# Queries' sums of squares by products with a column of ones, and an earlier load of the scan's levels, in a hybrid delta/SGU/Fourier step

## The chip, the cores and the metric

One Trainium2 chip, one core used. The metric is the device time of one execution in microseconds (us), the median of several runs.

## The reference

One layer of a flow-matching backbone on 2048 sample tokens and 128 prompt tokens, D_MODEL 1024. One input projection feeds three mixers of width 512: a gated delta rule (A, 4 heads of 128), a spatial gating unit (B) and a Fourier mix (C). Each is gated, projected, weighted by a sigmoid merge gate, summed and projected out. What the change touches is branch A:

```python
def l2norm(x):
    return x * lax.rsqrt(jnp.sum(x * x, axis=-1, keepdims=True) + EPS)
...
q = l2norm(q.reshape(B, T, H_A, DK)) * (DK ** -0.5)
k = l2norm(k.reshape(B, T, H_A, DK))
...
m = eye + bc[..., :, None] * jnp.einsum('bnhik,bnhjk->bnhij', kc, kc) * dec_strict
sol = lax.linalg.triangular_solve(m, rhs, left_side=True, lower=True, unit_diagonal=True)
def step(s, inp):
    u = u0_ - jnp.einsum('bhck,bhkv->bhcv', w_, s)
    o = jnp.einsum('bhck,bhkv->bhcv', qg_, s) + jnp.einsum('bhij,bhjv->bhiv', qk_, u)
    s = gl_[..., None, None] * s + jnp.einsum('bhck,bhcv->bhkv', kd_, u)
...
pb = jnp.einsum('btnw,nwd->btnd', br, w_branch)
merged = jnp.einsum('btnd,btnd->btd', gt, pb)
```

## The kernel before, in words

TensorE runs one long stream of matrix products: the input projection by column blocks, then the merges n = 1, 2, 0 of the three branches, then the output projection. Nearly all products are float16, each float32 operand split into a high and a low part and three products taken (`mm3`). Their instructions all stand on line 250.

Branch A is woven into that stream. `Pace` gives it a step whenever enough of the main stream has been issued. It works in chunks of 128 tokens, 17 in all, in 5 groups (the prompt's chunk, then four of four chunks):

- `prep` (lines 1007 to 1094, 437 to about 800 us in the profile) takes a chunk's q, k and v, which lie with the head's 128 channels on the partitions. It turns k, v and q by transposes on TensorE (line 1016; 4 of each, one for a head), sums squares over the channels on ScalarE (line 1022), takes the inverse root on GpSimd (line 1024), scales k into `tok`, turns `tok` back (line 1049), and makes the Gram matrices in float16.
- `base_inverse` (line 1101 on) inverts the 32 x 32 diagonal blocks of a group's triangular systems in 31 rounds between VectorE (line 1114, tile XB) and GpSimd (line 1115, tile E), then stores the result (`ei`).
- `scan` runs both directions over the chunks, 34 steps. For each chunk `level` builds the full inverse R from the 32-blocks: it loads `ei` into the tile ES and the Gram matrix into N and sn (lines 1171 to 1177, DMAs on SyncE's queue), and then multiplies in four steps: ES with N, ES with Q, T with sn, R with Q. ES, N and Q exist once and are shared by all levels. A step of the scan has its own products: S with the turned k (sk), v with R, u with k (kn), and those of the output (`attend`). Generators `lev` (the level of the next chunk), `nlev` (the one after) and `att` are advanced by `next` at fixed places of a step.

At the same time `gate_unit` finishes a block of branch B or C: a product on GpSimd (line 1465, tile st), a square on ScalarE (line 1466) and a store from GpSimd's queue (line 1467, br). Weights are converted ahead (lines 315, 327, 328: squares and both halves). In a merge, `branch_block` loads the branch's rows (tile st, three buffers) and converts them into `big` (lines 1691 and 1692).

The order of instructions on each engine is not that of the code: a scheduler with a model of the engines sorts them, so an edit at one place moves rows at others behind it. Names in rows read out<-moving, stationary for a product; a number behind a name is that of a buffer.

Of the kernel before, what the change touches and what calls it, by code (L numbers as in the profile page):

```python
# [14 lines left out]
AF = mybir.ActivationFunctionType  # L15
ALU = mybir.AluOpType
# [4 lines left out]
P = 128  # L21
# [6 lines left out]
H = 4  # L28
WB = 512
EPS = 1e-6  # L30
# [164 lines left out]
def hybrid_flow_kernel(ctx: ExitStack, tc: tile.TileContext, x_prompt, x_sample, state_delta, c, c_ctx, w_ada,  # L195
# [4 lines left out]
    G, V, A, PE = [_InTurn(tc, e_) for e_ in (nc.gpsimd, nc.vector, nc.scalar, nc.tensor)]  # L200
# [9 lines left out]
    def sb(pl, shape, tag, dt=F32, bufs=None):  # L210
        kw = {} if bufs is None else {"bufs": bufs}
        return pl.tile(list(shape), dt, tag=tag, name=nm(tag), **kw)
# [6 lines left out]
    ps_d = [pool(ctx, f"ps_d{i}", 1, space=PSUM) for i in range(3)]  # L219
# [4 lines left out]
    def bank(pl, shape, tag="b"):  # L224
        if pl is ps_d:
            rot[0] += 1
            pl = ps_d[rot[0] % 3]
        return pl.tile(list(shape), F32, tag=tag, name=nm(tag))
# [9 lines left out]
    ident, ones = K["ident"], K["ones"]  # L238
# [10 lines left out]
    def mm(out, l, r, start=True, stop=True, reopened=False):  # L249
        newest[0] = PE.matmul(out, l, r, start=start, stop=stop, skip_group_check=reopened)  # L250
# [453 lines left out]
    for ti, (t0, tn) in enumerate(TBS):  # L704
        g = 0 if t0 < NS else 1
# [13 lines left out]
        for k in range(KT):  # L719
            x, hi, _ = part_of(k)  # L720
# [91 lines left out]
    dq = pool(dl, "dqa", 1, side="right")  # L812
# [172 lines left out]
    def rows(part, t):  # L985
        x = sb(d2, [P, H, P], "kq" if part else "qr", bufs=3 if part else 2)
        SY.dma_start(x, qkvD[part * 4:part * 4 + 4, :, chunk_off(t):chunk_off(t) + P].rearrange("h p t -> p h t"))
        return x
# [18 lines left out]
    def prep(g, ci, t, nxt, held):  # L1007

        tok = sb(dq, [P, 2, WB], "tok")
        ss = sb(dq, [P, 2, H], "ss2", bufs=2)  # L1010
        cur = dict(held)

        def turned(part):
            ps = bank(ps_d, [P, WB])
            for h in range(H):
                PE.transpose(ps[:, hs(h)], cur[part][:, h, :], ident)
            return ps

        def norm(ps, i):
            sq = sb(dq, [P, WB], "sq")  # L1020
            for h in range(H):
                A.activation(sq[:, hs(h)], ps[:, hs(h)], AF.Square, accum_out=ss[:, i, h:h + 1])
            V.tensor_scalar(ss[:, i, :], ss[:, i, :], EPS, None, ALU.add)
            G.tensor_tensor(ss[:, i, :], ss[:, i, :], mhalf.to_broadcast([P, H]), ALU.pow)  # L1024

        def more(key, make):
            if nxt is not None:
                held[key] = make()

        more(1, lambda: rows(1, nxt))  # L1030
        ps = turned(1)
        norm(ps, 1)
        V.tensor_tensor(h3(tok[:, 0, :]), h3(ps), bc(ss[:, 1, :], P), ALU.mult)
        yield 1
        more(0, lambda: rows(0, nxt))
        A.activation(tok[:, 1, :], turned(2), AF.Copy, scale=us)
        norm(turned(0), 0)
        G.tensor_scalar(rq[:, t, :], ss[:, 0, :], P ** -0.5, None, ALU.mult)
        Q16 = sb(d2, [P, 2, WB], "q16", F16)
        qr = cur[0].rearrange("p h x -> p (h x)")  # L1040
        made = A.activation(Q16[:, 0, :], qr, AF.Copy, scale=qs)
        V.scalar_tensor_tensor(Q16[:, 1, :], qr, qs, Q16[:, 0, :], ALU.mult, ALU.subtract)
        late([(qTD[t], Q16)], made)
        yield 1
        G.dma_start(kvD[t], tok)
        T = sb(d2, [P, 2, WB], "T", F16)
        ps = bank(ps_d, [P, WB])
        for h in range(H):
            PE.transpose(ps[:, hs(h)], tok[:, 0, hs(h)], ident)
        made = A.activation(T[:, 0, :], ps, AF.Copy, scale=FS)  # L1050
        V.scalar_tensor_tensor(T[:, 1, :], ps, FS, T[:, 0, :], ALU.mult, ALU.subtract)
        more(2, lambda: rows(2, nxt))
        late([(kTD[t], T)], made)
        yield 1
        dc = cur["dc"]
        ps = bank(ps_d, [P, WB])
        pair = lambda t_, h: (t_[:, 0, hs(h)], t_[:, 1, hs(h)])
        for h in range(H):
            mm3(ps[:, hs(h)], pair(T, h), pair(T, h))
        nd = sb(d2, [P, 2, H, 32], "nd", bufs=2)  # L1060
        for d in range(2):
            n_ = sb(d2, [P, WB], "n32", bufs=3)
            for h in range(H):
                V.scalar_tensor_tensor(n_[:, hs(h)], ps[:, hs(h)], beta[:, d, t, h:h + 1], dc[:, d, hs(h)], ALU.mult, ALU.mult)  # L1064
            for B in range(4):
                A.copy(nd[32 * B:32 * B + 32, d], h3(n_)[32 * B:32 * B + 32, :, 32 * B:32 * B + 32])  # L1066
            n16 = sb(d2, [P, 2, WB], "n16", F16, bufs=4)
            made = A.activation(n16[:, 0, :], n_, AF.Copy, scale=FS)
            V.scalar_tensor_tensor(n16[:, 1, :], n_, FS, n16[:, 0, :], ALU.mult, ALU.subtract)
            late([(nD[d][t], n16)], made)  # L1070
            yield 1
        more("dc", lambda: decay_rows(nxt))
        for d in range(2):
            G.dma_start(ndD[g][d, ci].rearrange("h p i -> p h i"), nd[:, d])
        ps = bank(ps_d, [P, WB])
        for h in range(H):
            mm3(ps[:, hs(h)], pair(T, h), pair(Q16, h))
        for d in range(2):
            q_ = sb(d2, [P, WB], "n32", bufs=3)
            V.tensor_mul(q_, ps, dc[:, d, :])  # L1080
            p16 = sb(d2, [P, 2, WB], "n16", F16, bufs=4)
            made = A.activation(p16[:, 0, :], q_, AF.Copy, scale=1.0 / FS)
            V.scalar_tensor_tensor(p16[:, 1, :], q_, 1.0 / FS, p16[:, 0, :], ALU.mult, ALU.subtract)  # L1083
            late([(qkD[d][t], p16)], made)
            yield 1
# [171 lines left out]
    def scan():  # L1257
# [31 lines left out]
        for i_, (d, s_, t) in enumerate(order):  # L1289
# [18 lines left out]
            yield 1  # L1308
            next(att, None)
            yield 1  # L1310
            next(nlev, None)
            yield 1
            next(lev, None)
            yield 1
            next(att, None)
            yield 1
# [11 lines left out]
            split(u, v_)  # L1328
            yield 1
            next(nlev, None)  # L1330
            yield 1
            next(att, None)
            yield 1
# [18 lines left out]
                split(S216, S2, 1.0 / FS)  # L1352
            yield 1
            next(nlev, None)
            lev, nlev = nlev, level(*order[i_ + 2][::2]) if i_ < 32 else iter(())
            loaded = step_loads(i_ + 1)
            R3 = next(nlev, None)
            yield 1
            yield 1
            for _ in att:  # L1360
# [322 lines left out]

    def branch_block(n, s, t0, tn):

        for g in range(4):
            st = sb(ep, [P, tn], "st", bufs=3)
            SY.dma_start(st, obD[n][g, :, t0:t0 + tn])
            yield
            with behind_gate():  # L1690
                A.activation(o16[:, 0, g, t0:t0 + tn], st, AF.Copy, scale=s)  # L1691
            V.scalar_tensor_tensor(o16[:, 1, g, t0:t0 + tn], st, s, o16[:, 0, g, t0:t0 + tn], ALU.mult, ALU.subtract)  # L1692
# [490 lines left out]
```

## Time and profile before

| | |
|---|---|
| time, median of 3 runs | 2151.89 us (2148.55 to 2152.83) |
| profiled execution | 2150.54 us |
| its span | 2148.7 us, mean granted TensorE clock 0.99 |
| TensorE busy | 2085.8 us (97%) |
| VectorE busy | 1328.0 us (62%) |
| ScalarE busy | 1062.1 us (49%) |
| GpSimd busy | 840.1 us (39%) |

TensorE (PE) is busy nearly all the time; what is not its work is its idle time of some 60 us and the stretches in which its clock is granted at half. PEld is the load of the stationary operand, which overlaps the products. A busy share is an average over the whole span, so stages are read apart, by windows.

### The profile page before, as it was taken

The page shows a single profiled execution, that of the slowest core. Times are in us where ns is not written, and L with a number is a line of the kernel's source. Part 1 is how long each engine was busy: PE and PEld are TensorE (multiplying, and loading weights), DVE is VectorE, ACT ScalarE, POOL GpSimd, SP SyncE. Part 2 cuts the span into 40 slices and gives each one's busy share as a digit, 9 for nine tenths or more (in the row PEclk, how much of TensorE's full clock was granted, in tenths as well). Part 3 has the DMA queues.
Part 4 walks back from the last instruction along what each step waited for, and adds up shares of the span by engine and source line. Part 5 has one row for each costly group of instructions (what it writes and reads, how often), then busy time and mean ns, then how long its engine had stood idle before and what let it go on. Part 6 is the DMA issues. An engine that isn't in the chain of part 4 may idle for free.

```text
span 2148.7 us, 42636 instructions
## 1 busy us (share of the span) xinstructions
PE 2085.8 (97%) x16133; PEld 1198.8 (56%) x16133; DVE 1328.0 (62%) x2945; ACT 1062.1 (49%) x2457; POOL 840.1 (39%) x1089
## 2 busy tenths in 40 slices
PE   8999999999999999999899999999999999999997
PEld 4454444455555677787555655555655444444443
DVE  6656854388777786466655555766665564666245
ACT  5554744465656664455544445655554353443112
POOL 0321342225565555542322233255443234343464
PEclk9999999999999999999999999999999999999999
DMA  9525722177877743444655556866664645456852
GB/s 353 220 77 186 270 102 102 68 222 232 260 227 245 222 142 95 118 139 136 203 183 170 161 167 187 252 214 210 211 204 131 210 165 176 167 196 237 339 220 88
DMA packets 222909, 403.24 MB, mean 188 GB/s; under 512 B 39720, under 2 KB 109632, under 8 KB 219888
## 3 DMA queue, kind: packets, MB, share of 16 engines
q1 hardware_dynamic: 167664, 290.84, 42.3%
q0 software_dynamic: 15216, 65.89, 8.1%
q10 hardware_dynamic: 39824, 43.79, 6.0%
q8 instruction: 127, 2.08, 0.4%
q14 instruction: 78, 0.64, 0.1%
HBM read 258.19 MB, written 142.24 MB: 186 GB/s over the span
## 4 chain that ended last, share of the span: by engine, by line
PE 50%; DVE 8%; DMA 7%; POOL 3%; ACT 3%; issue 3%; SPq 0%; ACTq 0%; DVEq 0%; POOLq 0%
PE b L250 50%; DMA st<-br 2%; DMA pa<-pa 1%; DMA ES<-ei 1%; POOL E L1115 1%; DVE XB L1114 1%; DVE big L1692 1%; ACT nd L1066 1%; POOL ss L1024 1%; POOL st L1465 0%; ACT big L1691 0%; DVE n L1083 0%; DMA wst<-in_w_blk_dram 0%; DVE sg L476 0%; DVE n L1064 0%
## 5 line engine op out<-in xcount | busy, mean ns | idle before, releaser
L250 PE MATMUL b<-xh,whi 128*128 128x512 f16 (+1 forms) x1920 | 650.4, 348 | 2.9 <-DVE sg L1455 1.8
L250 PE MATMUL b<-xl,whi 128*128 128x512 f16 (+1 forms) x1920 | 650.6, 347 | 0.0
L250 PE MATMUL b<-xh,wlo 128*128 128x512 f16 (+1 forms) x1920 | 649.4, 347 | 0.0
L250 PEld LDWEIGHTS <-whi 128*128 128x128 f16 x3856 | 351.7, 98 | 322.6 <-issue 7.5
L250 PEld LDWEIGHTS <-wlo 128*128 128x128 f16 x1928 | 188.7, 98 | 176.7 <-issue 2.2
L250 PE MATMUL b<-big,bhi 128*128 128x512 f16 (+1 forms) x960 | 251.1, 347 | 1.7 <-ACT big L1691 1.1
L250 PE MATMUL b<-big,blo 128*128 128x512 f16 (+1 forms) x480 | 163.0, 347 | 0.0
L1735 POOL TENSOR_TENSOR mrow<-mrow,sg 128x512 f32<-128x512 f32 (+1 forms) x80 | 93.4, 1169 | 146.2 <-DVE sg L1734 115.4
L953 POOL TENSOR_TENSOR cy<-cy,raw 128x545 f32<-128x545 f32 (+1 forms) x48 | 64.4, 1368 | 183.6 <-ACT raw L952 183.6
L250 PEld LDWEIGHTS <-xh 128*128 128x128 f16 x1496 | 117.0, 98 | 28.8 <-issue 1.4
L250 PEld LDWEIGHTS <-bhi 128*128 128x128 f16 x960 | 86.7, 98 | 76.6 <-issue 2.6
L1115 POOL TENSOR_TENSOR E<-E,XB 128x31 f32<-128x31 f32 (+15 forms) x155 | 94.0, 607 | 84.6 <-DVE XB L1114 67.8
L250 PEld LDWEIGHTS <-xl 128*128 128x128 f16 x1068 | 98.1, 98 | 44.9 <-DMA tw<-tw 1.4
L1725 ACT ACTIVATE sg<-b,winv 128x512 f32<-128x512 f32 (+1 forms) x120 | 74.0, 616 | 94.0 <-PE b L250 93.4
L1188 POOL COPY T<-ES 32x256 f16<-32x256 f16 x68 | 32.1, 473 | 174.5 <-DMA ES<-ei 159.1
L250 PE MATMUL b<-whi,xh 128*128 128x128 f16 x544 | 92.7, 219 | 0.0
L250 PE MATMUL b<-whi,xl 128*128 128x128 f16 x544 | 92.7, 219 | 0.0
L250 PE MATMUL b<-wlo,xh 128*128 128x128 f16 x544 | 92.7, 219 | 0.0
L328 DVE SCALAR_TENSOR_TENSOR wlo<-wst,wsc,whi 128x1024 f16<-128x1024 f32 x52 | 69.9, 1346 | 31.4 <-ACT whi L327 31.1
L1295 POOL TENSOR_TENSOR skn<-skn,ed 128x512 f32<-128x512 f32 x34 | 37.2, 1095 | 122.5 <-DMA skn<-kv 122.5
L315 ACT ACTIVATE wlo<-wst 128x1024 f16<-128x1024 f32 x52 | 54.9, 1056 | 58.2 <-DMA wst<-in_w_blk_dram 54.8
L1114 DVE TENSOR_TENSOR XB<-XB,E 128x31 f32<-128x31 f32 (+15 forms) x155 | 55.3, 357 | 41.7 <-POOL E L1115 41.1
(532 smaller groups left out, 4314.8 us busy)
## 6 DMA issues: line engine op xcount, KB each, us to landing
wst<-in_w_blk_dram SPq DMA_DIRECT2D x58, 512.0 KB, 4.7
pa<-pa POOLq DMA_DIRECT2D x16, 896.0 KB, 4.4
qkv<-cy POOLq DMA_DIRECT2D x12, 1089.0 KB, 5.3
st<-br SPq DMA_DIRECT2D x48, 256.0 KB, 2.9
mrow<-mrg SPq DMA_DIRECT2D x16, 576.0 KB, 4.2
pa<-pa SPq DMA_DIRECT2D x5, 1792.0 KB, 11.9
dc<-dec SPq DMA_DIRECT2D x17, 512.0 KB, 4.7
kq<-qkv SPq DMA_DIRECT2D x34, 256.0 KB, 5.3
```

Of the source, the lines that this page charges most:

```text
L250: newest[0] = PE.matmul(out, l, r, start=start, stop=stop, skip_group_check=reopened)
L315: w.squared = A.activation(w.lo, st, AF.Square, accum_out=ss)
L328: w.low = V.scalar_tensor_tensor(w.lo, st, s, w.hi, ALU.mult, ALU.subtract)
L953: G.tensor_tensor(y[:, c0:c1], y[:, c0:c1], raw[:, 1 + c0:1 + c1], ALU.mult)
L1024: G.tensor_tensor(ss[:, i, :], ss[:, i, :], mhalf.to_broadcast([P, H]), ALU.pow)
L1066: A.copy(nd[32 * B:32 * B + 32, d], h3(n_)[32 * B:32 * B + 32, :, 32 * B:32 * B + 32])
L1114: V.tensor_tensor(t3, X3[:, 0:k, k:k + 1].to_broadcast([P, k, n_]), E3[:, k:k + 1, k:32].to_broadcast([P, k, n_]), ALU.mult)
L1115: G.tensor_tensor(E3[:, 0:k, k:32], E3[:, 0:k, k:32], t3, ALU.subtract)
L1188: G.tensor_copy(T16[rows(a0, b), :, :, b], ES[0:32, :, 2 * a0 + b, :, wT])
L1295: G.tensor_tensor(h3(kn_), h3(kn_), bc(ed[:, d, t, :], P), ALU.mult)
L1725: gated_[0] = A.activation(sg, ps, AF.Sigmoid, scale=gw.inv)
L1735: G.tensor_tensor(mr, mr, sg, ALU.add)
```

## The change: what it does

Three edits.

1. In `prep`, q is no longer turned. ScalarE squares the 512 columns of q as loaded, in one instruction, into `q2`. TensorE then multiplies each head's squares (as the stationary operand, float32) by one column of ones, which sums over the channels, into a PSUM tile of 128 x 4. VectorE reads the sums there. The squares of k are dumped into the still unused half of `tok` instead of a tile of their own.
2. In the scan's step, `next(lev)` comes ahead of `next(nlev)` at one place, and the level two chunks ahead is set up (its loads are issued) behind the split of u instead of at the step's end.
3. In `branch_block`, three rows are loaded at once, and the fourth after the first conversion.

```diff
         def norm(ps, i):
-            sq = sb(dq, [P, WB], "sq")
             for h in range(H):
-                A.activation(sq[:, hs(h)], ps[:, hs(h)], AF.Square, accum_out=ss[:, i, h:h + 1])
-            V.tensor_scalar(ss[:, i, :], ss[:, i, :], EPS, None, ALU.add)
+                A.activation(tok[:, 1, hs(h)], ps[:, hs(h)], AF.Square, accum_out=ss[:, i, h:h + 1])
+            inverse_root(ss[:, i, :], i)
+
+        def inverse_root(sums, i):
+            V.tensor_scalar(ss[:, i, :], sums, EPS, None, ALU.add)
             G.tensor_tensor(ss[:, i, :], ss[:, i, :], mhalf.to_broadcast([P, H]), ALU.pow)
...
+        qr = cur[0].rearrange("p h x -> p (h x)")
+        q2 = sb(dq, [P, WB], "sq")
+        A.activation(q2, qr, AF.Square)
         ps = turned(1)
         norm(ps, 1)
...
-        norm(turned(0), 0)
+        ps = bank(ps_d, [P, H])
+        for h in range(H):
+            mm(ps[:, h:h + 1], q2[:, hs(h)], ones[:, 0:1])
+        inverse_root(ps, 0)
...
+            next(lev, None)
+            yield 1
             next(nlev, None)
-            yield 1
-            next(lev, None)
...
             next(nlev, None)
+            later = level(*order[i_ + 2][::2]) if i_ < 32 else iter(())
+            R3 = next(later, None)
...
-            lev, nlev = nlev, level(*order[i_ + 2][::2]) if i_ < 32 else iter(())
+            lev, nlev = nlev, later
             loaded = step_loads(i_ + 1)
-            R3 = next(nlev, None)
...
-        for g in range(4):
+        def loaded(g):
             st = sb(ep, [P, tn], "st", bufs=3)
             SY.dma_start(st, obD[n][g, :, t0:t0 + tn])
-            yield
+            return st
+
+        sts = [loaded(g) for g in range(3)]
+        yield
+        for g in range(4):
+            if g == 1:
+                sts.append(loaded(3))
+            st = sts[g]
```

The scheduler moves rows elsewhere too. Three places matter below. In the steady scan the engines' rows stay nearly as they were, two groups of products changing places; the loads of ES stay where they were on SyncE's queue, since they wait for the products that read ES.

First, GpSimd's queue at the end of the last inverse before the scan (E are the rounds of the inverse, st and br the product and store of a branch block). Before:

```order
L1115 TENSOR_TENSOR E_9690<-E_9690,XB_9689 128x4x28
L1465 TENSOR_TENSOR st_10527<-sg_10172,yT_9570 128x512
L1465 TENSOR_TENSOR st_10531<-sg_10231,yT_9570 128x512
L1465 TENSOR_TENSOR st_10535<-sg_10329,yT_9570 128x512
L1115 TENSOR_TENSOR E_9690<-E_9690,XB_9689 128x3x29
L1467 DMA br_3917<-st_10527 128x512
L1467 DMA br_3917<-st_10531 128x512
L1467 DMA br_3917<-st_10535 128x512
L1115 TENSOR_TENSOR E_9690<-E_9690,XB_9689 128x2x30
L1465 TENSOR_TENSOR st_10567<-sg_10564,yT_9570 128x512
L1465 TENSOR_TENSOR st_10599<-sg_10596,yT_9570 128x128
L1115 TENSOR_TENSOR E_9690<-E_9690,XB_9689 128x31
```

After:

```order
L1122 TENSOR_TENSOR E_9622<-E_9622,XB_9621 128x4x28
L1122 TENSOR_TENSOR E_9622<-E_9622,XB_9621 128x3x29
L1122 TENSOR_TENSOR E_9622<-E_9622,XB_9621 128x2x30
L1122 TENSOR_TENSOR E_9622<-E_9622,XB_9621 128x31
L1473 TENSOR_TENSOR st_10459<-sg_10104,yT_9502 128x512
L1473 TENSOR_TENSOR st_10463<-sg_10163,yT_9502 128x512
L1473 TENSOR_TENSOR st_10467<-sg_10261,yT_9502 128x512
L1475 DMA br_3917<-st_10459 128x512
L1475 DMA br_3917<-st_10463 128x512
L1475 DMA br_3917<-st_10467 128x512
L1144 MEMSET R_1255_10436 128x1024
```

The last rounds now run together, and the branch products and stores follow them. On TensorE, the first product of ES and N stands some 11 us of work earlier than before.

Second, TensorE's queue at the end of the first level's products of ES and Q. Before, the second level's product of ES and N is next:

```order
L250 MATMUL b_10903<-ES_10512,Q_1274_10508 128x64
L250 LDWEIGHTS Q_1274_10508
L250 MATMUL b_10903<-ES_10512,Q_1274_10508 128x64
L250 LDWEIGHTS N_1275_10510
L250 MATMUL b_11169<-ES_10512,N_1275_10510 128x32
```

After, other products follow, and the second level's product of ES and N comes 124 products later:

```order
L250 LDWEIGHTS Q_1257_10440
L250 MATMUL b_10835<-ES_10444,Q_1257_10440 128x64
L250 LDWEIGHTS xl_95
L250 MATMUL b_10933<-whi_9606,xl_95 128x128
L250 LDWEIGHTS xh_94
L250 MATMUL b_10933<-whi_9606,xh_94 128x128
```

So between the last reader of the first ES and the first reader of the second, TensorE now has other work: 56 products of 128 columns of the main stream, 16 of 512 columns, 24 of 128 and 3 of 256 of the Fourier mix, 12 each of T with sn and R with Q, and one of a single column.

Third, ScalarE's queue at the start of the first merge (S is the split of the scan's state, blo the square of a branch weight). Before:

```order
L327 ACTIVATE bhi_13438<-wst_11441,wsc_13445 128x512
L1297 CAST kn_1551_13567<-skn_13530 128x512
L315 ACTIVATE blo_13787,bsums_93<-wst_13634 128x512
L1231 ACTIVATE S_1544_13513<-S_11074 128x512
L1725 ACTIVATE sg_13557<-b_13489,winv_12257 128x512
```

After:

```order
L327 ACTIVATE bhi_13381<-wst_11373,wsc_13388 128x512
L1304 CAST kn_1534_13499<-skn_13473 128x512
L1238 ACTIVATE S_1528_13456<-S_11006 128x512
L315 ACTIVATE blo_13730,bsums_93<-wst_13566 128x512
L1740 ACTIVATE sg_13489<-b_13432,winv_12189 128x512
```

S has moved ahead of the square of the weight.

1 line of the change is left out of this document (removed).

## The prediction

> **What bounds the kernel now.** I read the page's first and fourth parts first, to see which engine sets the time.
>
> ```profile
> PE 2085.8 (97%) x16133; PEld 1198.8 (56%) x16133; DVE 1328.0 (62%) x2945; ACT 1062.1 (49%) x2457; POOL 840.1 (39%) x1089
> PE 50%; DVE 8%; DMA 7%; POOL 3%; ACT 3%; issue 3%; SPq 0%; ACTq 0%; DVEq 0%; POOLq 0%
> ```
>
> TensorE works 97% of the span. Only two things can move the end: the amount of work that TensorE gets, and its idle time. The windows view shows where that idle time lies, and at what granted clock (the columns are the window, its length, then busy us of PE, PEld, DVE, ACT and POOL, then PEclk, the DMA share and GB/s).
>
> ```profile
> 437.00:795.00 358.00, 353.56 (x2762) 216.85 (x2761) 285.03 (x702) 224.74 (x687) 192.30 (x278) 1.00 0.71 224
> 795.00:895.00 100.00, 96.12 (x1314) 80.19 (x1314) 62.44 (x148) 43.89 (x95) 54.59 (x88) 0.98 0.36 104
> 895.00:965.00 70.00, 61.39 (x784) 48.96 (x783) 40.76 (x100) 34.18 (x84) 34.95 (x57) 0.90 0.46 135
> 1015.00:1085.00 70.00, 62.15 (x523) 36.92 (x522) 47.47 (x118) 39.66 (x88) 20.98 (x32) 0.95 0.66 208
> 1085.00:1340.00 255.00, 255.00 (x2338) 152.61 (x2336) 141.94 (x384) 117.15 (x287) 72.44 (x110) 1.00 0.55 169
> 1340.00:1420.00 80.00, 72.59 (x634) 42.74 (x632) 55.71 (x138) 52.67 (x136) 33.95 (x42) 1.00 0.75 235
> ```
>
> The reader is to see four places. The preparation of the delta rule runs from 437 to 795 with 4.4 us of idle time in 358. The scan starts at about 895: 8.6 us idle in 70, at a mean clock of 0.90, so about 7 us more are lost. The first merge starts at about 1015: 7.9 us idle at 0.95, some 3.5 us more lost. From 1085 to 1340 the scan runs with no idle at all, and at the change from the first merge to the second (1340 to 1420) 7.4 us are idle again. The waits view names what ended some of it (total, times, longest, in us).
>
> ```profile
> PE b L250 <- DMA ES<-ei: 5.9, 2, 3.7
> PE b L250 <- ACT S L1231: 4.0, 3, 2.3
> PE b L1049 <- DVE tok L1033: 2.7, 3, 1.5
> PE b L250 <- DVE sg L1455: 1.8, 1, 1.8
> PE b L250 <- ACT big L1691: 1.1, 2, 0.7
> ```
>
> **Part 1: the sums of squares of the queries.** Before, each of the 17 chunks turns q by four transposes, and ScalarE squares the result in four pieces. After, ScalarE squares q once, unturned, and TensorE multiplies the four heads' squares, as stationary operands, by one column of ones. First ScalarE's side, from the groups of line 1022 and, for one 512-column square, of line 1466:
>
> ```profile
> L1022 ACT ACTIVATE sq<-b x136: 252/277/337, 440.2 to 793.9; 128x128 f32<-128x128 f32 x136
> L1022 ACT ACTIVATION_READ_ACCUMULATOR sq<-b x136: 188/211/272, 440.3 to 794.1; 128x1 f32 x136
> L1466 ACT ACTIVATE sg<-st x40: 292/630/686, 553.8 to 1037.4; 128x512 f32<-128x512 f32 x32, 128x128 f32<-128x128 f32 x8
> ```
>
> ScalarE loses 4 × (0.277 + 0.211) = 1.95 us a chunk and gains 0.63, so 17 × 1.32 = 22 us of its busy time go. It was busy for 225 of the 358 us, so this is taken from an engine with slack. I count it at nothing directly; its indirect use is below. TensorE's side is what counts, since TensorE has no slack there:
>
> ```profile
> L1016 PE MATMUL b<-cst,qr x68: 272/273/279, 440.4 to 792.0; 128*128 128x128 f32 x68
> L182 PE MATMUL b<-cst,rs x34: 272/275/377, 21.2 to 131.1; 128*128 128x128 f32 x34
> 609.84 1.04 PE L1016 MATMUL b<-cst,kq 128*128 128x128 f32 x8
> 610.71 0.60 PE L1016 MATMUL b<-cst,qr 128*128 128x128 f32 x4
> 611.15 0.38 PE L250 MATMUL b<-xh,whi 128*128 128x512 f16 x1
> 164.92 0.84 PE L250 MATMUL b<-tok,cst 128*128 128x68 f32 x6
> 165.60 0.38 PE L250 MATMUL b<-xl,whi 128*128 128x512 f16 x1
> ```
>
> A transpose is one record (68 for 17 chunks of 4). A true float32 product is two: the spread of the root (line 182, tile rs) is one product a chunk, and has 34 records for 17. The durations of 0.27 us overlap, so I take the distance from start to start. Twelve transposes take 611.15 − 609.84 = 1.31 us, 0.109 each, so q's four cost 0.44. Six records of the float32 products at 164.92 take 0.68 us, 0.113 each, most of them with only 68 moving columns. Fewer columns did not make them cheaper, which points at the load of the 128 stationary columns as the limit. Four new products are eight records: 8 × 0.113 = 0.90. The difference is 0.46 us a chunk, and 17 × 0.46 = **+7.8 us** of work on TensorE. The low bound is 0, if a one-column record takes half as long as a 68-column one; a high one is +10, if a chain of such small products also leaves gaps of 0.1 us.
>
> The Trainium skill, on the page "TensorE: Matmul & The Clock Gate", section "LDWEIGHTS (loading the stationary operand)", speaks against this edit in the same way: the load of a stationary operand takes its columns divided by 1.2 GHz whatever the other side is, so 0.107 us for 128; by it the term would be 17 × (0.85 − 0.44) = 7.1 us, an estimate. The trace's 0.109 and 0.113 agree with it, and no run here shows a one-column float32 product.
>
> What cover is there? In this stretch 4.4 us of idle time exist. The waits on tok (2.7 in all, some of it just past 795) and on sg (1.8) belong to it. The new products stand between the transposes of k, which tok comes from, and the transposes of tok, so they fill about half a microsecond of each such wait; ScalarE's shorter queue brings the sums for k earlier. I take −2 us for both (0 to −4), and −1 for the clock right behind, which dips to 0.98 after 795 (0 to −2).
>
> **Part 2: the scan's levels.** In the steady scan (1085 to 1340) TensorE is never idle, and the new order there swaps two neighbouring groups of about 2 us. I count nothing (within ±1). At the start of the scan it is different:
>
> ```profile
> 900.65 0.18 PE L250 MATMUL b<-ES,N 128*128 128x32 f16 x1 [0.55 <-POOL T L1188]
> 906.13 0.28 PE L250 MATMUL b<-ES,Q 128*128 128x64 f16 x4
> 910.07 0.47 PE L250 MATMUL b<-ES,N 128*128 128x32 f16 x8 [3.66 <-DMA ES<-ei]
> 916.31 0.39 PE L250 MATMUL b<-v,R 128*128 128x128 f16 x2 [1.32 <-ACT R L1203]
> 937.12 0.45 PE L250 MATMUL b<-ES,N 128*128 128x32 f16 x8 [2.20 <-DMA ES<-ei]
> 925.22 1.22 PE L250 MATMUL b<-cf,X 128*128 128x128 f16 x19
> 926.28 0.38 PE L250 MATMUL b<-xh,whi 128*128 128x512 f16 x1
> 926.50 0.38 PE L250 MATMUL b<-xl,whi 128*128 128x512 f16 x1
> ```
>
> ES is one buffer. Its second load can only start when the products of ES and Q at 906 have read the first, and before the next product stands right behind them: hence 3.66 us. In the new order some 9.7 us of other products stand between: 16 of 512 columns at 0.215 us (926.28 to 926.50), three of half that width, and 105 narrow ones at 0.056 (19 in the 1.06 us from 925.22). That covers the 3.66. The 1.32 at v,R goes too, since R,Q now stands further ahead, and of the 2.20 perhaps half. So 6 of the 8.6 us can go.
>
> Against it stands the first product of all. It now comes about 11 us of TensorE work earlier, and what it needs does not come as much earlier:
>
> ```profile
> 869.95 3.75 POOL L1465 TENSOR_TENSOR st<-sg,yT 128x512 f32<-128x512 f32 x3 [0.54 <-DVE yT L1641]
> 876.45 1.69 POOL L1465 TENSOR_TENSOR st<-sg,yT 128x512 f32<-128x512 f32 x2 [0.51 <-DMA br<-st]
> 878.10 0.25 POOL L1115 TENSOR_TENSOR E<-E,XB 128x31 f32<-128x31 f32 x1
> 888.80 0.95 POOL L1137 MEMSET R<- 128x1024 f16 x1 [9.39 <-DMA ei<-XB]
> 894.71 2.55 SPq L1171 DMA_DIRECT2D ES<-ei  x3
> 899.76 0.83 POOL L1188 COPY T<-ES 32x256 f16<-32x256 f16 x2 [3.17 <-DMA ES<-ei]
> ```
>
> The chain is: the rounds of E on GpSimd end at 878.4, the store of ei is awaited for 9.39 us, six clears follow, ES is asked for at 894.7 and is there at 899.8. In the new order the rounds of E come ahead of the branch products that held them for 3.75 us from 869.95 on and for 1.69 from 876.45 on, each with the DMA issues behind it. That brings the chain 5 to 7 us forward. So the first product, 11 us earlier by work, waits 0.55 + 11 − 6, about 5 us. Net idle time: 8.6 − 6 + 4.5, about 7. The clock may gain more, since one wait replaces four in 40 us; of the 7 us lost to it I let 4.5 go. Together I take **−6 us** (from −12, where the chain gains all that the product does, to +3, where it gains nothing).
>
> The Trainium skill has a rule on the same page, "TensorE: Matmul & The Clock Gate", section "Part 1: The HAM clock gate": TensorE falls to half clock after about 3.4 us of idleness, so one wait of 5 us would be followed by a slow stretch. The 3.66 us wait with its mean clock of 0.90 agrees. It is the weight behind the second rival.
>
> **At the start of the first merge** the order changes as a by-product. ScalarE's queue there:
>
> ```profile
> 1030.96 0.63 ACT L315 ACTIVATE blo<-wst 128x512 f16<-128x512 f32 x1 [3.03 <-DMA wst<-in_w_brb_dram]
> 1032.25 0.22 PE L250 MATMUL b<-S,sk 128*128 128x128 f16 x1 [2.27 <-ACT S L1231]
> ```
>
> The scan's state S stood behind a weight conversion that waited 3.03 us for its transfer. In the new order S comes ahead of it, and the 2.27 us go. The other waits in this stretch are of 0.1 to 1.5 us and will fall anew. I take −2.5 (from −6, where the clock's 3.5 us lost there go too, to +4).
>
> **Part 3: the branch tiles.** There were and are three buffers. The waits view of line 1691 shows what the conversions wait for:
>
> ```profile
>   DMA st<-br: 33.6, 26
> ```
>
> ScalarE waits 33.6 us, but TensorE waits for it only 1.1 us (above). A load can still start only when a buffer is free, and in the new order SP's rows for these loads are almost where they were. I take −0.3 (from −1.1 to +1). At the change between merges (1340 to 1420) the end of the scan is now interleaved with the conversions a little differently: 0, from −3 to +4.
>
> **The sum** is +7.8 − 2 − 1 − 6 − 2.5 − 0.3 = −4.0. The profiled execution took 2150.54 us, with 2148.7 of span, so it gives 2146.5. The median shown is 1.35 us above the profiled run; half of that added gives **2147 us**. That is 0.2% under the median, at the border of what a measurement of this kernel can tell from no change (0.2%, 4.3 us).
>
> **The rivals.** Forecast (chance 0.42): as above, its own range 2143 to 2151. About half of it is faster by over 0.2%, half within.
>
> Slower: the first product's wait (0.28). TensorE pays the full +7.8 at 437 to 795, and at the scan's start the first product's wait takes back what the others give: if the chain to ES comes forward by 2 us and not 6, this wait is 9.5 us, idle time becomes 8.6 − 6 + 9, about 11.6, and the clock's loss stays at 7. That is +3 there, −2 at the waits in preparation and the merge at 0: 2150.5 + 7.8 + 3 − 2, about 2159. It decides from the point where the chain gains less than 4 us. For it: each wait on SP or the stores can hold the chain, and the store of ei alone took 9.39. Against it: the order on GpSimd is plainly better.
>
> Faster (0.18): one-column products are cheap (+3 and not 7.8), or the chain gains all, and the clock recovers in both places. By the low ends of parts 2 and the merge: 7.8 − 3 − 12 − 6, about −13, so 2137.
>
> The edits do nothing that shows (0.12): the products' time and the gains cancel, 2150 to 2154.
>
> **How the numbers follow.** Faster by over 0.2%: 0.22 of the forecast's 0.42, and 0.18, so 0.40. Within: 0.20 and 0.09, so 0.29. Slower: 0.28 and 0.03, so 0.31. The range takes in both rivals' centres and leaves their far halves out: 2137 to 2160.
>
> **What would show it.** The trace of after should have 136 records of one column for q's sums, about 0.9 us of TensorE's time a chunk, and everything behind 795 should stand 4 to 6 us later against the same work. The second product of ES and N should wait under 1 us, the first 3 to 7. The S of the first merge should not wait behind blo. I am wrong if the records of one column stand closer than 0.08 us, if the first ES,N waits over 9 us, or if new waits of over 4 us appear between 1340 and 1420 or in the steady scan.

## The result, and the profile after

The change took 2159.71 us (median of 5, 2156.57 to 2161.46) against 2150.58 for the kernel before: a ratio of 1.0046, 95% interval 1.0036 to 1.0057. It is about 9 us slower, where 4 us faster was forecast. A second comparison on another occasion gave 1.0033 (1.0021 to 1.0045), about 7 us. The profiled execution took 2156.57 us, the lowest of the five, with a span of 2154.7. The first part of its page:

```profile
PE 2093.9 (97%) x16201; PEld 1204.5 (56%) x16201; DVE 1331.9 (62%) x2945; ACT 1054.4 (49%) x2338; POOL 852.1 (40%) x1089
```

TensorE has 68 more records (136 products' records in place of 68 transposes) and is busy 8.1 us longer; ScalarE is relieved of only 7.7 us of busy time, where 22 were forecast. The forecast added up the durations of the squares and of the readings of their sums (66 us for the 272 records of line 1022), but these overlap: before, they kept ScalarE busy for 38.9 us in the preparation. In the change k's half takes 20.0 and the new squares of q 10.7.

To see where the time went, I cut both traces at the same pieces of work and not at the same times: the preparation (from the first turn of k to the last turn of tok), the scan's start (to the first product of the first merge), scan and merges (to the scan's last product of v and R), and the end. The windows view of before, then of the change, with these cuts:

```profile
439.53:797.45 357.92, 352.24 (x2764) 216.73 (x2763) 284.35 (x700) 224.13 (x687) 194.75 (x281) 1.00 0.70 222
797.45:1040.87 243.42, 226.53 (x3023) 183.17 (x3022) 153.62 (x385) 118.43 (x281) 114.74 (x184) 0.96 0.43 128
1040.87:1627.47 586.60, 574.68 (x5126) 341.59 (x5124) 357.20 (x910) 311.72 (x807) 208.82 (x282) 1.00 0.63 195
1627.47:2136.80 509.33, 507.05 (x2706) 243.25 (x2703) 266.69 (x547) 173.83 (x318) 210.41 (x209) 1.00 0.55 197
```

```profile
438.84:805.57 366.73, 359.24 (x2834) 224.34 (x2833) 285.01 (x707) 218.68 (x570) 206.26 (x287) 1.00 0.69 217
805.57:1042.25 236.68, 222.44 (x3021) 179.32 (x3020) 150.59 (x379) 116.41 (x279) 112.12 (x177) 0.97 0.45 132
1042.25:1628.53 586.28, 578.64 (x5124) 343.39 (x5122) 362.01 (x910) 311.70 (x806) 210.98 (x283) 0.99 0.63 195
1628.53:2142.89 514.36, 510.06 (x2707) 244.45 (x2705) 267.66 (x547) 173.97 (x318) 210.40 (x209) 0.99 0.55 195
```

The lengths differ by +8.8, −6.7, −0.3 and +5.0 us; with −0.7 before the first cut that is +6.1, the difference of the two profiled executions. The preparation loses 8.8: 7.0 of TensorE's busy time (359.24 − 352.24) and 1.8 of idle time. The scan's start gives 6.7 back: 4.1 of busy time for nearly the same products (226.53 − 222.44), at a higher granted clock, and 2.7 of idle time. In scan and merges the idle time falls by 4.3 and the busy time rises by 4.0, so that almost nothing is left. The end loses 5.0 (3.0 busy, 2.0 idle), where nothing was forecast.

**The new products.** Their timeline in one chunk, and what followed them:

```profile
612.55 1.04 PE L1016 MATMUL b<-cst,kq 128*128 128x128 f32 x8
613.43 0.95 PE L250 MATMUL b<-cst,sq 128*128 128x1 f32 x8
614.24 0.38 PE L250 MATMUL b<-xh,whi 128*128 128x512 f16 x1
```

Eight records take 614.24 − 613.43 = 0.81 us: the second starts 0.03 behind the first, and the other seven distances, the one to the next float16 product among them, are 0.112. Against 0.44 for the transposes that is 0.37 a chunk, 6.3 us for 17; the busy time of the stage shows 7.0. One moving column is as dear as 68 (0.112 us a record against 0.113).

**The preparation's waits.** The waits view of the change, and then the timeline of ScalarE's queue at 475 us:

```profile
PE b L250 <- ACT st L1534: 4.0, 2, 2.9
PE b L1056 <- DVE tok L1038: 0.9, 1, 0.9
```

```profile
475.16 1.06 ACT L315 ACTIVATE wlo<-wst 128x1024 f16<-128x1024 f32 x1 [4.69 <-DMA wst<-in_w_blk_dram]
476.21 0.70 ACT L1534 ACTIVATE st<-sg,vss 128x512 f16<-128x512 f32 x1
```

The waits on tok fell from 2.7 to 0.9 us, and those on sg in this stage went, as forecast. But a new one came: the spatial gating unit's conversion st stood behind a weight's square that waited 4.69 us for its transfer, and TensorE stood for 2.9 us behind st.

**The scan's start.** The last round of the inverse on GpSimd, the first clear, and TensorE's first product of ES and N:

```profile
877.94 0.25 POOL L1122 TENSOR_TENSOR E<-E,XB 128x31 f32<-128x31 f32 x1 [0.30 <-DVE XB L1121]
888.91 0.95 POOL L1144 MEMSET R<- 128x1024 f16 x1
901.94 0.45 PE L250 MATMUL b<-ES,N 128*128 128x32 f16 x8 [3.50 <-DMA N<-n]
```

The rounds end at 878.2 and the clear starts at 888.9: the same times as before (878.35 and 888.8), although all work before them ended 8 us later. So the chain came forward by 8 us against TensorE's work (from 80.9 to 72.6 us behind the end of the preparation). The first product waited 3.5 us, by the profile for N and no longer for ES, and the waits of 3.66, 1.32 and 2.20 us behind it are gone. But in this stage TensorE now waited 3.0 us for the tile xc, which had cost it 0.3 before.

**The first merge.** S does come ahead of the weight's square now (1030.35 against 1032.35 us):

```profile
1030.35 0.63 ACT L1238 ACTIVATE S<-S 128x512 f16<-128x512 f32 x1 [1.40 <-DVE S L1352]
1032.35 0.63 ACT L315 ACTIVATE blo<-wst 128x512 f16<-128x512 f32 x1 [1.38 <-DMA wst<-in_w_brb_dram]
1032.16 0.77 PE L250 MATMUL b<-S,sk 128*128 128x128 f16 x11 [0.74 <-DVE S L1239]
1034.66 0.51 PE L250 MATMUL b<-R,Q 128*128 128x64 f16 x12 [1.56 <-DVE Q L1226]
1037.78 0.80 PE L250 MATMUL b<-S,sq__1557_13670 128*128 128x128 f16 x6 [1.27 <-DVE o L1255]
```

The 2.27 us wait became 0.74, but R,Q (1.56) and S with sq (1.27) waited in its place. Two more cuts, from a product of ES and N ahead of this place to one behind it, show the opening of the merge as a whole, before and then after:

```profile
1008.22:1148.97 140.75, 131.90 (x1205) 79.98 (x1202) 89.95 (x235) 72.10 (x167) 39.92 (x64) 0.98 0.61 189
```

```profile
1009.59:1153.79 144.20, 135.97 (x1222) 82.48 (x1220) 91.14 (x236) 72.33 (x168) 41.13 (x64) 0.95 0.61 187
```

It did not gain 2.5 us, it lost 3.5. The loss is busy time at a lower granted clock (0.95 and not 0.98); about 1 us of it may be the 17 small products that the new order moved in here (an estimate, at 0.056 us each).

**The end.** One wait for the output weights, before and then after:

```profile
1999.11 2.76 PE L250 MATMUL b<-tw,xl 128*128 128x512 f16 x12 [0.96 <-DMA tw<-tw]
```

```profile
2003.92 4.37 PE L250 MATMUL b<-tw,xl 128*128 128x512 f16 x12 [2.22 <-DMA tw<-tw]
```

The wait is 1.3 us longer, and the twelve products behind it take 4.37 us and not 2.76, for they ran in part at half clock (0.50 is the granted clock here):

```profile
2006.00:2008.30 2.30, 2.30 (x7) 0.85 (x6) 0.00 (x0) 0.00 (x0) 0.00 (x0) 0.50 1.03 420
```

The same happened at 1714 us, where the wait for sg was 2.08 and not 1.09 us. In the second profiles of both kernels (below) the slow products behind the wait for tw were there again (a wait of 2.02 us in the change and 0.70 before, 4.45 us for the twelve products). The loss at 1714 was not: there the waits were 1.23 and 1.67 us, at full clock.

### The profile page after: what moved, and what is told of

Read it like the earlier page. It is cut to its first block, busy times and chain, and to the rows that moved or that the text cites. A ratio compares the mean times of both kernels' runs of the same rounds, so it can differ in the third digit from the quotient of the medians.

```text
span 2154.7 us, 42639 instructions
## 1 busy us (share of the span) xinstructions
PE 2093.9 (97%) x16201; PEld 1204.5 (56%) x16201; DVE 1331.9 (62%) x2945; ACT 1054.4 (49%) x2338; POOL 852.1 (40%) x1089
## 3 DMA queue, kind: packets, MB, share of 16 engines
q8 instruction: 127, 2.08, 0.4%
## 4 chain that ended last, share of the span: by engine, by line
PE 46%; DVE 7%; DMA 6%; ACT 3%; POOL 3%; issue 2%; SPq 1%; ACTq 0%; DVEq 0%; POOLq 0%
PE b L250 45%; DMA st<-br 2%; POOL E L1122 1%; DVE XB L1121 1%; DMA tw<-tw 1%; DMA wst<-in_w_blk_dram 1%; DMA ei<-XB 1%; ACT nd L1073 0%; DVE big L1707 0%; DMA skn<-kv 0%; DVE wlo L328 0%; POOL ss L1026 0%; PE b L1389 0%; DMA sq__1354_11599<-qT 0%; ACT big L1706 0%
## 5 line engine op out<-in xcount | busy, mean ns | idle before, releaser
L327 ACT ACTIVATE whi<-wst,wsc 128x1024 f16<-128x1024 f32 x52 | 59.4, 1143 | 41.4 <-DVE wsc L278 39.9
```

What stands on the lines that cost most here:

```text
L327: w.made = A.activation(w.hi, st, AF.Copy, scale=s)
```

## The experiments

Theories: W, the loss is TensorE's added work in a full stage. S, the scan's edit makes it. O (later called R), any new order of the preparation makes new waits. In the fences below the columns are those of the windows view again.

**Edit 1 alone.**

```diff
-        norm(turned(0), 0)
+            mm(ps[:, h:h + 1], q2[:, hs(h)], ones[:, 0:1])
```

> Edit 1 alone (queries' sums by products with ones; scan and branch tiles as before). Theory W (TensorE's work): the eight records of 0.112 us a chunk in place of four of 0.109 cost 17 x 0.46 = 7.8 us in a stage in which TensorE is full, so +5 to +10 us against before at the end of the preparation, less what the scan's start gives (the rounds of the inverse run together here too); 0.1 to 0.5% slower. Theory S (the scan's edit makes the loss): within 0.15% of before. Theory O (any new order makes new waits of some us at the stage changes): anything from -4 to +10, with the difference in waits and not in the preparation.

1.0049 (1.0030 to 1.0068). All of the loss is there without edits 2 and 3. Preparation, then the scan's start:

```profile
438.98:807.30 368.32, 361.70 (x2835) 225.33 (x2834) 284.66 (x707) 218.60 (x570) 206.12 (x287) 0.99 0.68 216
807.30:1046.19 238.89, 223.89 (x3021) 181.01 (x3019) 152.14 (x380) 116.54 (x279) 112.63 (x178) 0.96 0.44 131
```

The scan's start is 4.5 us shorter than in the first profile of before and 2.4 shorter than in the second (below), so a part of that gain comes without the scan's edit.

**Edits 2 and 3 without edit 1**, twice.

```diff
+            next(lev, None)
             next(nlev, None)
-            next(lev, None)
...
+            later = level(*order[i_ + 2][::2]) if i_ < 32 else iter(())
```

> Edits 2 and 3 without edit 1 (q turned and squared as before). Theory W: TensorE's work is that of before and the scan is full, so within 0.15% of before, or faster. Theory S: +6 to +10 us. Theory O: from -4 to +6 with new waits at the change of stages; up to the scan's start the order is that of before, so the scan's start keeps its idle time of 8 us.

> Edits 2 and 3 without edit 1 once more, to see if their small gain holds: 0.9975 to 1.0 of before if it does; above 1.0005 if it was chance. By theory W it has before's work and so the time of before or a little less, since the second wait for ES at the scan's start is shorter.

0.9991 (0.9981 to 1.0000), then 0.9985 (0.9974 to 0.9995). Theory S falls. This is the best version seen, 2 to 3 us faster than before and faster than the change. Where it gains, in the second run (the four windows):

```profile
440.61:798.97 358.36, 352.23 (x2764) 216.94 (x2763) 283.94 (x700) 224.12 (x687) 194.89 (x281) 1.00 0.70 222
798.97:1038.74 239.77, 223.42 (x3022) 180.13 (x3021) 152.17 (x386) 117.24 (x281) 113.42 (x183) 0.97 0.43 130
1038.74:1621.77 583.03, 574.06 (x5124) 341.47 (x5121) 360.00 (x910) 312.31 (x806) 211.34 (x283) 1.00 0.63 196
1621.77:2131.53 509.76, 507.58 (x2708) 243.36 (x2705) 267.46 (x547) 173.85 (x318) 210.51 (x209) 1.00 0.55 197
```

The preparation is that of before; the scan's start and the merges are 3.7 and 3.6 us shorter than in the first profile of before (1.6 and 2.1 shorter than in the second). Edit 3 by itself moves a single row, one load of st on SyncE's queue by two places, and was not run alone.

**The change with squares and ones in bfloat16.**

```diff
-        q2 = sb(dq, [P, WB], "sq")
+        q2 = sb(dq, [P, WB], "sq", BF16)
...
-            mm(ps[:, h:h + 1], q2[:, hs(h)], ones[:, 0:1])
+            mm(ps[:, h:h + 1], q2[:, hs(h)], ones16[:, 0:1])
```

> All three edits, but the squares and the column of ones in bfloat16 (the sums of squares are rounded coarser): four records a chunk at about 0.056 us in place of eight at 0.112. Theory W: 17 x (0.90 - 0.22) = 11 us of TensorE's work less than the change, so 9 to 12 us faster than it and 0 to 4 us faster than before. Theory S: as slow as the change, +6 to +10. Theory O: between -6 and +6 against before, by its own waits.

1.0005 (0.9993 to 1.0017): 0.41% or 9 us less than the change by its first comparison, 0.28% or 6 us by its second. Theory W had 9 to 12. Nor is it faster than before, where theory W had 0 to 4 us. One chunk's products, and the preparation:

```profile
614.42 0.24 PE L250 MATMUL b<-ones,sq 128*128 128x1 bf16 x4
614.52 0.38 PE L250 MATMUL b<-xh,wlo 128*128 128x512 f16 x1
```

```profile
439.99:798.55 358.56, 348.22 (x2765) 211.16 (x2763) 285.64 (x705) 217.69 (x569) 204.37 (x284) 1.00 0.70 222
```

Four products take 0.10 us. TensorE has 4.0 us less to do than before, and the stage is as long: idle time went from 5.7 to 10.3.

**The change with the weights' squares that come later in the code held behind the gating unit's conversion**, which removes most of the new wait at 477 us.

```diff
+        normed = A.activation(v2[:, 0], vn, AF.Copy, scale=ss)
+        if t == 7:
+            sgu_[0] = normed
...
-        with behind_gate():
+        with (tc.issue_after(sgu_[0].ins) if sgu_[0] is not None and not queued[0] else behind_gate()):
             w.squared = A.activation(w.lo, st, AF.Square, accum_out=ss)
```

> The change, with one weight's square held on ScalarE's queue behind the conversion of the spatial gating unit's chunk 7, ahead of which it waited 4.69 us for its transfer. Theory Q (that queue order made the new wait of 2.9 us in the preparation): the wait at 477 us goes, 2 to 3.5 us less than the change, 1.0025 to 1.004 of before. Theory W alone (only TensorE's work counts): as the change, 1.004 to 1.005.

1.0045 (1.0032 to 1.0058): nothing gained. The preparation, and its waits up to 660 us:

```profile
439.72:806.62 366.90, 359.82 (x2835) 224.42 (x2834) 285.64 (x707) 218.11 (x570) 204.77 (x287) 1.00 0.69 217
```

```profile
PE b L250 <- DVE T L1058: 1.2, 1, 1.2
PE b L1056 <- DVE tok L1038: 1.1, 1, 1.1
PE b L250 <- DVE vrow L1563: 0.9, 1, 0.9
PE b L250 <- ACT st L1534: 0.8, 1, 0.8
```

The named wait fell from 4.0 to 0.8 us, and T, tok and vrow, which TensorE had not waited for up to 660 us in the change, came next. The stage is as long as before the repair (366.90 to 366.73).

**More work and nothing else**: q's transposes done twice in each chunk, three times, and twice in every second chunk.

```diff
+        turned(0)
         norm(turned(0), 0)
```

> Before, with q's four transposes of each chunk done twice (the first result unused): 17 x 0.44 = 7.4 us more work on TensorE in the preparation and nothing else. Theory W: +5 to +9 us against before, like edit 1. Theory S: within 0.1% if such work were hidden. Theory O: -4 to +12.

> Before, with q's four transposes of each chunk done three times (two results unused): 17 x 0.88 = 14.8 us more work on TensorE in the preparation. Theory W (added work of the stage counts in full): 12 to 16 us slower, 1.0055 to 1.0075. Theory R (the reordering that any edit of this stage causes costs some 10 us, whatever the work): 9 to 12 us slower as with one extra turn, 1.004 to 1.0055.

> The same with one extra turn in every second chunk only: 8 x 0.44 = 3.5 us more work; its order on every engine differs from that of before about as much as that of the others does, and the rounds of the inverse run together here too. Theory W: 2 to 5 us slower, 1.001 to 1.0025. Theory R: 9 to 12 us slower, 1.004 to 1.0055.

1.0056 (1.0043 to 1.0069), 1.0124 (1.0106 to 1.0141) and 1.0069 (1.0054 to 1.0084): 12, 27 and 15 us for 7.4, 14.8 and 3.5 us of work, more than either theory had for the last two. Their preparations, in that order:

```profile
438.27:803.11 364.84, 359.52 (x2832) 224.82 (x2831) 290.48 (x705) 224.48 (x681) 204.50 (x286) 1.00 0.69 218
```

```profile
438.85:819.87 381.02, 369.04 (x2889) 232.99 (x2888) 288.50 (x706) 225.50 (x687) 200.61 (x287) 0.99 0.66 209
```

```profile
438.73:812.51 373.78, 361.19 (x2796) 221.90 (x2795) 289.58 (x703) 223.81 (x681) 197.86 (x285) 0.99 0.67 213
```

Added work is never hidden: busy time rises by 7.3, 16.8 and 9.0 us (some of the last two at half clock). But idle time is 5.3, 12.0 and 12.6 us and does not follow the work; the smallest edit has the most. That last profile is of the slowest of its six executions (2170.01 us, median 2163.14), so its share of idle time may be too high; but by the medians too the smallest edit costs more than the one with twice its work. Theory W alone, with 2 to 5 us for the last, falls; both act.

**No added work**: k's squares dumped elsewhere, and q's sums taken one step earlier.

```diff
-                A.activation(sq[:, hs(h)], ps[:, hs(h)], AF.Square, accum_out=ss[:, i, h:h + 1])
+                A.activation(sq[:, hs(h)] if i == 0 else tok[:, 1, hs(h)], ps[:, hs(h)], AF.Square, accum_out=ss[:, i, h:h + 1])
```

```diff
+        norm(turned(0), 0)
         yield 1
...
-        norm(turned(0), 0)
```

> Before with the squares of k dumped into the unused half of tok, as the change does, and nothing else: no engine's work changes, the order does (544 differing rows on TensorE). Theory W (loss = added work): within 0.15% of before. Theory R (a new order of the preparation costs by itself): 2 to 12 us slower, all of it idle time in the preparation.

> Before with q's transposes and squares taken one step earlier, ahead of v's: no engine's work changes, the order does (1753 differing rows on TensorE). Theory W: within 0.15% of before. Theory R: 2 to 12 us slower, idle time in the preparation and at the scan's start.

1.0025 (1.0014 to 1.0037) and 1.0016 (1.0007 to 1.0025): 5 and 3 us for no added work. The preparations:

```profile
437.80:802.70 364.90, 354.37 (x2765) 216.70 (x2763) 284.13 (x700) 224.21 (x687) 197.36 (x281) 1.00 0.69 218
```

```profile
438.25:799.02 360.77, 353.38 (x2765) 217.08 (x2763) 284.46 (x701) 224.48 (x687) 204.56 (x282) 1.00 0.69 221
```

They are 7.0 and 2.9 us longer than before, in executions that lie some 3 us under their medians. The first of these edits is a part of edit 1, and it is not a change of order alone. The half of `tok` is unused by its own chunk, but the pool holds one buffer of `tok` (line 812), so k's squares now have to wait until the chunk before has been stored from it. The profile has one such wait of ScalarE, of 1.4 us for kv<-tok; in the change it is 0.3. The second edit needs q one step earlier. So these runs show what edits without added work cost, and not what order alone costs; the change without this part of edit 1 was not run.

**No sums for q at all.**

```diff
-        norm(turned(0), 0)
+        V.tensor_scalar(ss[:, 0, :], ss[:, 1, :], 1.0, None, ALU.mult)
```

> Before without q's sums of squares: no transposes of q and no squares, k's sums are used in their place, so that q is not normalised by its own length. 17 x 0.44 = 7.4 us of TensorE's work and 33 us of ScalarE's less. Theory W (the stage follows TensorE's work both ways): 6 to 8 us faster. Theory B (another chain bounds it on that side, and removed work becomes idle time): 0 to 3 us faster, with idle time in the preparation up from 5.7 us by as much as the work falls.

1.0001 (0.9991 to 1.0011). Preparation, then the scan's start:

```profile
437.75:790.54 352.79, 346.01 (x2699) 209.61 (x2698) 287.85 (x703) 207.99 (x552) 183.96 (x267) 1.00 0.71 226
790.54:1033.93 243.39, 226.57 (x3020) 182.70 (x3019) 151.42 (x384) 117.61 (x279) 112.53 (x181) 0.95 0.44 129
```

In the profiled execution, 2146.1 us, the preparation is 5.1 us shorter, with 6.8 us of idle time where before had 5.7. But over all executions (median 2149.61) nothing is left, neither theory W's 6 to 8 us nor idle time that took the work's place, as theory B has it. Which stage loses it in the others stays open. At least, less work in this stage is worth less than more work costs.

**GpSimd's order at the scan's start**, forced by hand: the branch products held behind the rounds of the inverse, on edits 2 and 3, and on the bfloat16 version.

```diff
+        with (tc.issue_after(eround_[0].ins) if eround_[0] is not None else ExitStack()):
-        G.tensor_tensor(o, sg, src, ALU.mult)
+            G.tensor_tensor(o, sg, src, ALU.mult)
```

> Edits 2 and 3 without edit 1, with the branch products held on GpSimd's queue behind the last rounds of the inverse, as the change has them. Theory G (the scan's start gained from that order on GpSimd): the start's idle time falls from some 16.9 us to 13 to 14 and its clock's loss by 2 to 4, 4 to 7 us faster than before, 0.997 to 0.998. Theory O (the start's gain was chance): within 0.1% of before.

> All three edits with the squares and the ones in bfloat16, and GpSimd's queue as in the last. Theory G: 4 to 7 us faster than the same kernel without that, 0.997 to 0.998 of before. Theory W with a full TensorE would add 3.7 us more. Theory O: within 0.1% of before.

1.0037 (1.0023 to 1.0051) and 1.0002 (0.9990 to 1.0014). Preparation and scan's start of the first:

```profile
439.44:804.05 364.61, 355.14 (x2765) 217.40 (x2763) 290.43 (x700) 223.88 (x687) 194.69 (x281) 1.00 0.69 218
804.05:1050.46 246.41, 226.07 (x3023) 181.78 (x3021) 155.35 (x386) 116.78 (x281) 112.90 (x183) 0.96 0.42 127
```

And the end of the rounds:

```profile
878.38 0.25 POOL L1116 TENSOR_TENSOR E<-E,XB 128x31 f32<-128x31 f32 x1 [0.30 <-DVE XB L1115]
```

The rounds end 74.6 us behind the preparation (878.63 − 804.05), against 80.9 before and 72.6 in the change: the order does bring the chain forward. Yet the scan's start is longer (246.4 us), not shorter. With the bfloat16 version the forced order brings the end of the rounds from 79.5 to 72.1 us, and the scan's start is 238.7 us against 239.1 without it. So theory G falls: this order on GpSimd does not shorten the stage by itself. The hold also acted on earlier groups and made the preparation 6.7 us longer, so whether the order has a share in the change's gain is not shown.

**Both kernels once more**, for a second profile.

> The change itself once more, for a second profile and on the chip of the others. Theory W: 1.0035 to 1.0055 again; the waits in the preparation stand at the same places, and what differs between executions lies in the start, in the first merge and in the clock, not in the preparation's work.

> The kernel before once more, against itself, for a second profile. All theories: within 0.1% of before. It shows how far two executions of one program differ, stage by stage.

1.0033 (1.0021 to 1.0045) and 0.9994 (0.9985 to 1.0003). Preparation and scan's start, of the change and then of before:

```profile
438.44:804.47 366.03, 359.36 (x2835) 224.43 (x2833) 283.88 (x707) 218.62 (x570) 205.88 (x287) 1.00 0.69 217
804.47:1041.52 237.05, 221.03 (x3021) 178.20 (x3019) 151.51 (x379) 116.11 (x279) 110.11 (x177) 0.98 0.44 131
```

```profile
439.59:797.91 358.32, 352.25 (x2764) 216.88 (x2763) 284.03 (x700) 224.16 (x687) 194.83 (x281) 1.00 0.70 222
797.91:1039.24 241.33, 225.43 (x3022) 181.92 (x3020) 153.72 (x385) 118.34 (x281) 114.85 (x184) 0.96 0.44 130
```

The preparation repeats within 0.7 us, and its added busy time is 7.1 us and was 7.0. The scan's start of before differs by 2.1 us between its two executions, so the change's gain there is 4 to 7 us.

## Why the prediction was wrong

TensorE's time between the same pieces of work, as forecast and as the difference of the profiles (us; the first merge's opening is 1008 to 1149 us in the profile of before):

| stage | forecast | first profiles | second profiles |
|---|---|---|---|
| up to the preparation | 0 | −0.7 | −1.1 |
| preparation | +7.8 − 2 | +8.8 | +7.7 |
| scan's start, to 1008 us | −1 − 6 | −6.7 | −4.0 |
| first merge's opening | −2.5 | +3.5 | +5.3 |
| rest of scan and merges | −0.3 | −3.8 | −1.4 |
| end | 0 | +5.0 | +2.9 |
| sum | −4.0 | +6.1 | +9.4 |

- **The products' cost, +7.8 us, was right.** By the rows it is 6.3 to 7.0. It was not hidden, and the bfloat16 version, which takes nearly all of it away, is 6 to 9 us faster than the change. The Trainium skill's rule for the load ("TensorE: Matmul & The Clock Gate", section "LDWEIGHTS (loading the stationary operand)"), which gives an estimate of 0.107 us for 128 columns, fits the 0.112 of float32; it does not fit the bfloat16 products, below. (The 7.1 us worked out from it in the prediction are 7.0 by the figures printed there.)
- **The step that failed first is "I take −2 us for both".** The waits on tok and sg shrank as argued, but I counted only waits that the trace of before showed. Its order has little idle time in this stage, 5.7 and 6.1 us in two executions; the other orders have 5.3 to 12.7. A new order could hardly gain there and could lose, and two edits without added work lost 3 and 5 us. In place of −2 the change's idle time in this stage rose by 1.8 and 0.8 us (7.49 against 5.68, 6.67 against 6.07).
- **The scan's start, −6, was right in size and in its parts.** To 1008 us TensorE's busy time falls by 4.4 and 4.2 us for nearly the same products, where 4.5 were forecast for the clock; the idle time changes by −2.3 and +0.2, where −1.5 was forecast. The chain came forward by 8 us, where 5 to 7 were forecast. That this is the cause is not shown: the same order, forced, brought the chain forward by 6.3 us and shortened nothing, and the doubled transposes, whose rounds end 71.4 us behind the preparation, had a scan's start of 245.8 us. Versions with the scan's edit and without that order were shorter there than before (edits 2 and 3 by 1.6 to 3.7 us in their second run, the bfloat16 version by 2.2 to 4.3). Which edit carries the gain is not settled.
- **The first merge, −2.5, missed by the most**: +3.5 and +5.3 for its opening. S came ahead and its wait shrank by 1.5 us, but R,Q and S with sq were late next, and the products ran at a lower clock. I had named no successor. With edit 1 alone the opening took 141.0 us, as before (140.8), and with edits 2 and 3 alone 142.0 and 143.8: at least a part of this loss goes with edits 2 and 3.
- **The end, counted at nothing, failed**: +5.0, and +2.9 between the second profiles. A wait of about 1 us that was in the trace of before grew to 2.0 to 2.2 in both, a second one in one of them, and products behind them ran at half clock.
- **The branch tiles, −0.3, were a gain for another reason.** TensorE's waits for big did not shrink: 1.1 us before, 2.4 and 3.4 in the change, and 3.5 with edit 1 alone, so edit 3 did not lengthen them. The rest of scan and merges gained all the same, with edits 2 and 3 alone too (2.4 and 4.9 us against the first profile of before); in the change the idle time there falls from 8.7 to 4.7 and from 9.0 to 7.3 us. What gave it was not taken apart.
- **The rival "slower" gave 2159 us for a reason that did not occur**: it needed a first wait of 9.5 us at the scan's start. Its true content was its first half, the full price of the products. That its sum meets the measured time, and that the time lies just inside the slow end of the stated range, is luck.
- **None of the three signs by which I would have been wrong occurred.** The records stand 0.112 us apart, the first product of ES and N waited 3.5 us, and no new wait of over 4 us came where I looked for one. The signs watched the places where the loss was not; only the end of the preparation, 8 us later and not 4 to 6, showed it.

So the sum was +7.8 of cost and −11.8 of gains, of which the scan's start was there, and a gain of 1.4 to 3.8 us in the merges that was not forecast. What these gave went again into new waits and half clock: 1 to 2 us in the preparation, 3.5 to 5.3 in the first merge's opening, and 3 to 5 at the end. About the price of the products is left as the loss. How it divides between work and order in a single execution is a matter of which profile is read. That the loss is there with edit 1 alone, that the products without most of their price are 6 to 9 us faster, and that edits without added work cost 3 to 5 us, is shown. What order alone costs, apart from the wait on `tok`, and why the end became slower, stays open.

## What to carry to other kernels

On an engine that is full in a stage, count an edit's work on it in full, and count the gains from vanishing waits only if you can say what is late next: here most of the named waits that were removed had a successor. Where a scheduler sorts the whole program, an edit without any added work can cost a good part of what the one under test costs (3 and 5 us of 7 to 9 here); an order with little idle time can hardly improve and can easily get worse, so widen the range by that much, mostly on the slow side. Ask of a tile that looks unused how many buffers it has, and who still reads the last one. Undo the parts one by one: the two edits that did not touch the full stage were a small gain, hidden by the one that did.

## What the runs showed of the hardware

A bfloat16 product of 128 stationary columns with one moving column followed the one before it after 0.025 us; a float32 one, two records of 0.112, takes nine times as long. The Trainium skill, on the page "TensorE: Matmul & The Clock Gate", section "Weight-path perf modes — Fast Weight Load (FWL) and DoubleRow", says that the fast load of weights is on for 128 weights that are not float32 and gives about a factor of two. The load's own record agrees, with 0.192 us for float32 and 0.096 for bfloat16. But the distance from record to record differs by 4.5 (0.112 to 0.025 us), since the bfloat16 loads overlap more, and it is the distance that TensorE's time went by here.

A wait of 2.0 to 2.2 us was already enough, in some places, for some 3 us of half clock behind it (the twelve products at 2003.92 took 1.6 us longer). Waits of 1.23 and 1.67 us for sg at the other place were not. But the length of the wait does not settle it: the wait of 2.9 us for st at 477 us was followed by full clock in the change and by half clock with edit 1 alone, as the windows behind it show, in that order:

```profile
476.90:480.40 3.50, 2.92 (x22) 1.67 (x23) 3.45 (x7) 2.81 (x12) 0.00 (x0) 1.00 0.25 75
```

```profile
476.90:480.40 3.50, 3.11 (x16) 1.75 (x17) 3.50 (x8) 2.71 (x11) 0.00 (x0) 0.50 0.25 75
```
